# First weight sums of the down projections made in DRAM, and three more seven-product pairs

## The chip, the cores and the metric

The kernel runs on one core of one Trainium2 chip. The metric is the device time of one execution in microseconds (us); of several runs the median is given. A profile is one further execution, taken by the hardware profiler; its times are counted from the first instruction of the program. Engines: PE is TensorE (matmuls; PEld its weight loads), DVE is VectorE, ACT is ScalarE, POOL is GpSimd, SP is SyncE, which here only issues DMAs.

## The reference

A two-layer encoder trunk on 256 tokens of width 2048, in float32. Each layer has an attention sub-layer (token mixer and memory heads, one output projection) and an MLP:

```python
for i in range(DEPTH):                       # 2 layers
    h = rms_norm(x, norm_attn[i])
    ...                                      # input projection w_in_a or w_in_b, memory k/v, heads
    x = x + heads @ w_out[i]
    h = rms_norm(x, norm_mlp[i])
    x = x + jnp.square(jax.nn.relu(h @ w_up[i])) @ w_down[i]
```

`w_up` is 2048 x 8192 and `w_down` 8192 x 2048. The change concerns the product with `w_down`, and when its preparations are done.

## The kernel before, in words

**Products in three parts.** Every weight and every activation is split into a high part (a cast to float32r on ACT) and a low part (the difference, on DVE); a product is three matmuls: high x high, high x low, low x high. `split` (L411 to L413) is used for weights, activations and sums alike, so most of ACT's and DVE's work stands on L412 and L413.

**Pieces.** All weights come in pieces of 512 KB (128 partitions x 1024 floats) in the order of `plan`: layer by layer the input projection (`a` with 10 chunks of 8 pieces, `b` with 6), the memory projection (16 pieces), `out` (32), `up` (16 chunks of 8 pieces) and `down` (two halves of the output columns, each 32 pairs of 2 pieces). `piece` hands out the next piece and calls `fetch` so that two more are under way (AHEAD). `fetch` issues the load on SP (L389) into one of four raw buffers, and splits into one of four hi and four lo buffers. The framework's scheduler then puts each engine's instructions into an order at build time; at run time every engine works through its own in order, held up by semaphores.

**Pairs with seven products.** In `out` and `down` a pair of pieces is normally 8 groups of three matmuls (2 k-blocks x 2 token halves x 2 column chunks; `one_of_eight`). For the pairs listed in FAST (15 of 32), or LATE (13 of 32; layer 0, second half), `seven` does the same work in 7 groups, by Strassen's scheme. It needs sums of weight blocks: the first sum `a` (one block plus another broadcast over two, 128 x 1024) and two further halves `b` (L344, L345), which are then split like weights (`sum_pair`). It also needs differences of activations (`differences`, L515 to L518). These are made once for each hidden block j during `up`, saved to DRAM on GpSimd's queue by `keep` (tile `kept`), and loaded back on GpSimd's queue when pair j comes (L1038 in before).

**Where the first sums come from in before.** For 19 of the 58 fast pairs (MADE, MADE_LATE) `make_sum` makes the first sum ahead, during the first 13 chunks of `up`: three loads on SP (768 KB) into h2 and t2k tiles, the sum on DVE (L282, tile h), and a save of 512 KB in two parts on GpSimd's queue (L307, tile `madesum`). Such a pair later loads its sum (`big<-madesum`, L327) and only the half of the second piece that it still needs (`t2k<-in_w_down`). For the other 39 pairs `sum_pair` makes the sum on DVE (L282, big<-big) when the pair is fetched.

**Slots and the wait chains.** During `down`, raw pieces, first sums and second sums of the fast pairs live in six slots of one large tile (`big`). These are free once the hidden blocks of chunks 6 to 11 (AWAY) that were in them have been saved to DRAM on GpSimd's queue (tile `hid`, L987) and their differences taken. Loads into slots are issued on SP up to two pairs ahead (L324, L327, L333), in the same queue as all other weight loads. `bias_hot` (L796) gathers rows of a table on GpSimd's queue early in layer 0: eight groups of four DMAs, each read by DVE (L797) and then by matmuls (L806) that build the bias of the attention scores.

Of the kernel before, what the change touches and what calls it, by code (L numbers as in the profile page):

```python
# [22 lines left out]
P = 128  # L23
# [21 lines left out]
SINGLE = 4  # L45
AHEAD = 2
WARM = 10
FAST = (1, 3, 5, 7, 9, 11, 13, 15, 17, 19, 21, 23, 25, 27, 29)
LATE = (3, 5, 7, 9, 11, 13, 15, 17, 19, 21, 23, 25, 27)
AWAY = range(6, 12)  # L50
LATE_BLK = (9, 13, 17, 21, 25)
LOOK = 2
KEEP_AFTER = (2, 6)
MADE_GAP = 1
MADE = (3, 9, 15, 21, 27)
MADE_LATE = (7, 13, 19, 25)
LAM_INIT = 0.8 - 0.6 * math.exp(-0.3 * 0)

G_ATTN, G_MEM, G_MLP = 0, 2 * KT, 4 * KT
# [9 lines left out]
def trunk(ctx: ExitStack, tc: tile.TileContext, xin, xtok, memin, memtok, posrel, gcol, rows,  # L69
# [172 lines left out]
            return LATE if (name, h) == ("down0", 1) else FAST  # L242
        return ()

    def made_pairs(name, h):

        if name.startswith("down"):
            return MADE_LATE if (name, h) == ("down0", 1) else MADE
        return ()

    def plan_pairs(name, n):
        plan.extend((name, h, j) for h in range(2) for j in range(2 * n))

# [27 lines left out]
    def first_sum(a, first, upper):  # L281
        nc.vector.tensor_tensor(a, first.rearrange("p (a n) -> p a n", a=2), upper.unsqueeze(1).broadcast_to([P, 2, 512]), op=ALU.add)  # L282

    def make_sum(name, h, j):

        box = {}

        def load(i):
            if i == 0:
                box["raw"] = quad("h2", (P, 1024), F32), t2k([P, 512])  # L290
            first, upper = box["raw"]
            with tc.issue_after(behind[0].ins):
                if i < 2:
                    nc.sync.dma_start(first[:, i * 512:(i + 1) * 512], weights[name][h, 2 * j][:, i * 512:(i + 1) * 512])
                else:
                    nc.sync.dma_start(upper, weights[name][h, 2 * j + 1][:, 512:1024])

        def add():
            first, upper = box["raw"]
            box["a"] = quad("h2", (P, 2, 512), F32)  # L300
            box["kept"] = dp.tile([P, 2, 512], F32, name=nm("madesum"))
            first_sum(box["a"], first, upper)
            made_in[name, h, j] = box["kept"]
            save(0)

        def save(i):
            nc.gpsimd.dma_start(box["kept"][:, i, :], box["a"][:, i, :])  # L307

        return Task([lambda: load(0), lambda: load(1), lambda: load(2), add, lambda: save(1)], gap=MADE_GAP)

    made_in = {}
    hidden_in, hids = {}, {}
# [80 lines left out]
    def piece(name, c, j, lead=None):  # L393

        if lead is not None:
            fetch(2, lead)
            if j == 7:
                for _ in range(AHEAD):
                    fetch()
        else:  # L400
            while plan and len(ready) <= AHEAD:
                fetch()
        key, hi, lo = ready.popleft()
        assert key == (name, c, j), (key, name, c, j)
        return hi, lo

    def split_gain(hi, lo, src, g):
# [544 lines left out]
    def mlp(layer, X2, last):  # L952
# [13 lines left out]
            kept[j] = dp.tile([P, 2, 512], F32R, name=nm("kept"))  # L966
            nc.gpsimd.dma_start(kept[j], t2)

        to_make = [(f"down{layer}", h, j) for h in range(2) for j in made_pairs(f"down{layer}", h)]
        for c in range(16):  # L970
            for i in range(len(to_make) * c // 13, len(to_make) * (c + 1) // 13):
                if i < len(to_make):
                    make_sum(*to_make[i])
            ps = chunk_out(f"up{layer}", c, 8, lambda k: X2[k], "mm" if c % 2 == 0 else "aux", 2 if c == 0 else 1)
            if c == 0:
                mlp_stats()
            ht = wide[:, c - 6] if 6 <= c < 12 else blk([P, 4, S], F32)
            for o in range(4):
                t = t1k()
                nc.scalar.copy(t, ps[o][:, 256:512])  # L980
                nc.vector.tensor_tensor(t, ps[o][:, 0:256], t, op=ALU.add)
                nc.vector.scalar_tensor_tensor(ht[:, o, :], t, 0.0, t, op0=ALU.max, op1=ALU.mult)
            hT.append(ht)
            if c in AWAY:
                for i in range(2):
                    hidden_in[2 * c + i] = dp.tile([P, 512], F32, name=nm("hid"))
                    nc.gpsimd.dma_start(hidden_in[2 * c + i], hidden(2 * c + i))  # L987
            for j in (2 * c, 2 * c + 1):
                if any(j in fast_pairs(f"down{layer}", h) for h in range(2)):
                    Task([Light(lambda j=j: keep(j), 0)], wait=KEEP_AFTER[j % 2])  # L990
        N2 = Halves()

        def h2_of(j):
            t2 = quad("h2", (P, 2, 512))
# [5 lines left out]
        for half_ in range(2):  # L1000
            tag = "mm" if half_ == 0 else "aux"
            ps = [[bank(tag) for _ in range(2)] for _ in range(2)]
            chunks = (2 * half_, 2 * half_ + 1)
            fast = fast_pairs(f"down{layer}", half_)

            def add_to(n, t, src, i=0):
                at = chunks[n] * 512 + i
# [20 lines left out]
            for j in range(32):  # L1028
# [11 lines left out]
                else:  # L1040
                    for kk in range(2):
                        for t in range(2):
                            for n in range(2):
                                own_last = 2 * fast[-1] - 1 if last and half_ == 1 and n == t == 1 else 4 * KT - 1
                                one_of_eight(ps, n, t, 2 * j + kk, own_last, two, at)
                if j == fast[-1]:
                    shared(side, add_to)
# [45 lines left out]
    rows_done = [Task([lambda i=i: bias_hot(i), lambda i=i: bias_rows(i, bias)], [prep], wait=BW, gap=BGAP) for i in range(8)]  # L1093
    Task([lambda: bias_save(bias)], rows_done)
    H2 = Halves(lambda pair: "h2" if pair < 6 else "x2")
    loads = Task([lambda c=c: load_residual(c) for c in range(4)], wait=RES_AT, gap=RES_GAP, front=True)
    for g in range(3):
        if g == 2:
# [29 lines left out]
    st1 = cp.tile([P, 4], F32, name="st1")  # L1128
    H2 = Halves(lambda pair: "h2" if pair < 6 else "x2")
    bias = bias_load()  # L1130
    ps = chunk_tok("b", 3, X2, steps=2)
    row_stats(st1)
    kT, kd = norm_T(ps, st1, 4, gc[:, G_BK:G_BK + 1])
# [82 lines left out]
```

## Time and profile before

| what | value |
|---|---|
| median of 3 runs | 2094.53 us (2094.41 to 2095.34) |
| span of the profiled execution | 2092.7 us |
| median of the runs less that span | 1.8 us |
| granted TensorE clock, mean | 1.000 |
| matmul records, busy share of PE | 10920, 100% |
| busy share of DVE, ACT, POOL | 78%, 56%, 5% |
| DMA moved | 506.29 MB, mean 242 GB/s |

The groups of the page name line, engine, operation, written tile <- read tiles with shapes, count, busy time in us, mean ns of one, idle time before them and what ended it. The rows of the stages give for a stretch of the span the busy time of each engine, the granted clock, the mean busy share of the 16 DMA engines and the rate they moved. A wait row names who waited, for whom, the total in us, the number and the longest. Roughly: layer 0's input and memory projections with the heads run to about 320 us, then `out` to 414 us, `up` to 772 us, `down` to 1103 us; layer 1's to about 1308, 1403, 1761 and 2090 us.

### The profile page before, as it was taken

The numbers are of one execution on the slowest core, as the hardware profiler recorded it, in microseconds if no ns is written. First come the engines' busy times: TensorE is split into PE (matmuls) and PEld (weight loads), VectorE is DVE, ScalarE is ACT, GpSimd is POOL, SyncE is SP. The second block draws the span as 40 slices with busy tenths as digits, with TensorE's granted clock in tenths as the row PEclk, the third lists the DMA queues.
The fourth block names the chain that finished last, engine by engine and source line by source line (L and its number), as shares of the span: only waits on it lengthen the run. The fifth ranks groups of instructions, "written<-read, shape, count | busy, mean of one in ns | idle before, by whom it ended". The sixth has DMA issues, their size and how long they took to land.

```text
span 2092.7 us, 30004 instructions
## 1 busy us (share of the span) xinstructions
PE 2088.2 (100%) x10920; PEld 1773.8 (85%) x10920; DVE 1640.3 (78%) x2467; ACT 1173.6 (56%) x1776; POOL 103.0 (5%) x193
## 2 busy tenths in 40 slices
PE   9999999999999999999999999999999999999999
PEld 8888888888888888888888888888888888888887
DVE  7667778866666679999986677886676667999998
ACT  7467665544444456666655566564444445666664
POOL 1200000000011000000000000000010100000000
PEclk9999999999999999999999999999999999999999
DMA  9666654577789778878866555457788877888884
GB/s 320 241 204 200 194 161 161 186 241 251 251 298 310 238 264 274 293 246 268 303 243 197 178 171 178 149 194 250 252 272 299 307 231 277 273 288 289 284 294 145
DMA packets 150995, 506.29 MB, mean 242 GB/s; under 512 B 17856, under 2 KB 18880, under 8 KB 150592
## 3 DMA queue, kind: packets, MB, share of 16 engines
q1 hardware_dynamic: 131536, 437.78, 63.1%
q0 software_dynamic: 19168, 66.60, 9.5%
q8 instruction: 85, 1.39, 0.3%
q14 instruction: 62, 0.51, 0.1%
q10 hardware_dynamic: 144, 0.01, 0.0%
HBM read 466.96 MB, written 37.36 MB: 241 GB/s over the span
## 4 chain that ended last, share of the span: by engine, by line
PE 100%; DVE 0%; issue 0%
PE mm L478 11%; PE aux L478 11%; PE mm L465 7%; PE mm L466 7%; PE mm L467 7%; PE mm L505 7%; PE mm L506 7%; PE mm L504 7%; PE aux L506 7%; PE aux L505 7%; PE aux L504 7%; PE mm L482 6%; PE aux L482 6%; PE aux L600 1%; PE aux L577 1%; PE aux L619 1%
## 5 line engine op out<-in xcount | busy, mean ns | idle before, releaser
L413 DVE TENSOR_TENSOR lo<-raw,hi 128x1024 fp32r<-128x1024 f32 (+1 forms) x616 | 738.6, 1210 | 365.3 <-ACT hi L412 361.0
L412 ACT CAST hi<-raw 128x1024 fp32r<-128x1024 f32 (+1 forms) x616 | 632.0, 1040 | 592.4 <-PE mm L478 158.2
L465 PE MATMUL mm<-hi,x 128*128 128x512 f32 x640 | 256.5, 403 | 0.0
L466 PE MATMUL mm<-lo,x 128*128 128x512 f32 x640 | 251.3, 393 | 0.0
L467 PE MATMUL mm<-hi,x 128*128 128x512 f32 x640 | 250.4, 392 | 0.2 <-DVE x L409 0.2
L478 PE MATMUL mm<-x,hi 128*128 128x512 f32 x1024 | 246.9, 391 | 0.0
L478 PE MATMUL aux<-x,hi 128*128 128x512 f32 x1024 | 246.9, 391 | 0.0
L478 PEld LDWEIGHTS mm<-x,hi 128*128 128x128 f32 x1024 | 188.3, 188 | 36.3
L478 PEld LDWEIGHTS aux<-x,hi 128*128 128x128 f32 x1024 | 188.3, 188 | 36.3
L412 ACT CAST x<-big 128x1024 fp32r<-128x1024 f32 x106 | 110.6, 1053 | 141.6 <-DVE big L345 114.9
L504 PE MATMUL mm<-hi,h 128*128 128x512 f32 (+1 forms) x454 | 176.1, 388 | 0.0
L505 PE MATMUL mm<-lo,h 128*128 128x512 f32 (+1 forms) x454 | 176.0, 388 | 0.0
L506 PE MATMUL mm<-hi,h 128*128 128x512 f32 (+1 forms) x454 | 176.0, 388 | 0.0
L504 PE MATMUL aux<-hi,h 128*128 128x512 f32 x440 | 171.5, 390 | 0.0
L506 PE MATMUL aux<-hi,h 128*128 128x512 f32 x440 | 171.2, 390 | 0.0
L505 PE MATMUL aux<-lo,h 128*128 128x512 f32 x440 | 171.2, 389 | 0.0
L467 PEld LDWEIGHTS mm<-hi,x 128*128 128x128 f32 x640 | 120.3, 188 | 26.3 <-DVE x L409 0.5
L465 PEld LDWEIGHTS mm<-hi,x 128*128 128x128 f32 x640 | 120.6, 189 | 23.8
L466 PEld LDWEIGHTS mm<-lo,x 128*128 128x128 f32 x640 | 120.8, 189 | 23.0 <-DVE lo L413 1.0
L482 PEld LDWEIGHTS aux<-x,lo 128*128 128x128 f32 x1024 | 131.3, 191 | 5.0
L482 PEld LDWEIGHTS mm<-x,lo 128*128 128x128 f32 x1024 | 131.1, 191 | 4.8
L482 PE MATMUL mm<-x,lo 128*128 128x256 f32 x1024 | 133.0, 283 | 0.0
(270 smaller groups left out, 3101.8 us busy)
## 6 DMA issues: line engine op xcount, KB each, us to landing
raw<-in_w_up SPq DMA_DIRECT2D x256, 512.0 KB, 4.6
raw<-in_w_down SPq DMA_DIRECT2D x140, 512.0 KB, 4.7
big<-in_w_down SPq DMA_DIRECT2D x97, 512.0 KB, 5.0
raw<-in_w_a SPq DMA_DIRECT2D x72, 512.0 KB, 3.7
h<-kept POOLq DMA_DIRECT2D x58, 512.0 KB, 6.0
raw<-in_w_out SPq DMA_DIRECT2D x52, 512.0 KB, 4.0
raw<-in_w_b SPq DMA_DIRECT2D x48, 512.0 KB, 3.7
raw<-in_w_mem SPq DMA_DIRECT2D x32, 512.0 KB, 3.6
```

The source lines that it names most:

```text
L412: nc.scalar.copy(hi, src)
L413: return nc.vector.tensor_tensor(lo, src, as32(hi), op=ALU.subtract)
L465: nc.tensor.matmul(ps[t], lhsT=xh, rhs=hi[:, ws], start=(k == 0), stop=False)
L466: nc.tensor.matmul(ps[t], lhsT=xh, rhs=lo[:, ws], start=False, stop=False)
L467: nc.tensor.matmul(ps[t], lhsT=xl, rhs=hi[:, ws], start=False, stop=(k == KT - 1))
L478: nc.tensor.matmul(ps[o], lhsT=hi[:, cols(k % 2, o)], rhs=x2.rearrange("p a s -> p (a s)"), start=(k == 0), stop=(k == 2 * nj - 1))
L482: nc.tensor.matmul(ps[o][:, 256:512], lhsT=lo[:, cols(k % 2, o)], rhs=x2[:, 0, :], start=False, stop=False)
L504: nc.tensor.matmul(acc_, lhsT=x(0), rhs=w2[0][:, ws], start=first_, stop=False)
L505: nc.tensor.matmul(acc_, lhsT=x(0), rhs=w2[1][:, ws], start=False, stop=False)
L506: nc.tensor.matmul(acc_, lhsT=x(1), rhs=w2[0][:, ws], start=False, stop=last_)
L577: nc.tensor.transpose(out=pt[:, h * P:(h + 1) * P], in_=qn[t][:, h * P:(h + 1) * P], identity=ident)
L600: nc.tensor.transpose(out=pt[:, kt * S + qt * P:kt * S + (qt + 1) * P], in_=p_of(qt)[:, kt * P:(kt + 1) * P], identity=ident)
```

## The change

`make_sum`, its lists and its tasks go. `make_sums(layer)`, called at the start of each layer's input projection, lays down a list of steps, one every 5 consumed pieces before `up` and one every 10 in `up`, starting 26 pieces (layer 0) or 2 pieces (layer 1) after the call. A step issues two DMAs on GpSimd's queue: an add for the pair before, and a copy for the next pair. The copy goes from the weights in DRAM to a tile in DRAM (512 KB); the add reads half a piece twice (a broadcast, 512 KB in all) and adds it to the copy by the DMA's own accumulation. Each copy is given a dependency on the low-part split of the piece fetched last. All 61 fast pairs of the two down projections now find their first sum in DRAM; `sum_pair` makes one on DVE only for `out`. FAST gets 16 pairs in place of 15, with 9 and 10, and 18 and 19, next to each other; LATE stays. `own_last` is now worked out from the last pair that is not fast (28 in both kernels).

```diff
-FAST = (1, 3, 5, 7, 9, 11, 13, 15, 17, 19, 21, 23, 25, 27, 29)
+FAST = (1, 3, 5, 7, 9, 10, 12, 14, 16, 18, 19, 21, 23, 25, 27, 29)
 LATE = (3, 5, 7, 9, 11, 13, 15, 17, 19, 21, 23, 25, 27)
...
-MADE_GAP = 1
-MADE = (3, 9, 15, 21, 27)
-MADE_LATE = (7, 13, 19, 25)
+SUM_AT = {0: 26, 1: 2}
+SUM_GAP = 5
+SUM_GAP_UP = 10
...
+    def make_sums(layer):
+
+        name = f"down{layer}"
+
+        def copy(h, j):
+            made_in[name, h, j] = dp.tile([P, 2, 512], F32, name=nm("madesum"))
+            after_piece(nc.gpsimd.dma_start(made_in[name, h, j].rearrange("p a n -> p (a n)"), weights[name][h, 2 * j]))
+
+        def add(h, j):
+            upper = weights[name][h, 2 * j + 1][:, 512:1024]
+            nc.gpsimd.dma_start(made_in[name, h, j], upper.unsqueeze(1).broadcast_to([P, 2, 512]), accum_op=ALU.add)
+
+        def after_piece(ins):
+            tc.add_manual_dep(ins.ins, done[0].ins.name, mybir.DependencyInfo(mybir.DependencyClass.Sync, mybir.DependencyReason.DATA),
+                              reason="behind a piece")
+
+        def step(i):
+            if i:
+                add(*wanted[i - 1])
+            if i < len(wanted):
+                copy(*wanted[i])
+
+        wanted = [(h, j) for h in range(2) for j in fast_pairs(name, h)]
+        at = fetched[0] + SUM_AT[layer]
+        for i in range(len(wanted) + 1):
+            making.append((at, lambda i=i: step(i)))
+            at += SUM_GAP if at < before_up[layer] else SUM_GAP_UP
...
         key, hi, lo = ready.popleft()
         assert key == (name, c, j), (key, name, c, j)
+        fetched[0] += 1
+        while making and making[0][0] <= fetched[0]:
+            making.popleft()[1]()
         return hi, lo
...
-        to_make = [(f"down{layer}", h, j) for h in range(2) for j in made_pairs(f"down{layer}", h)]
         for c in range(16):
-            for i in range(len(to_make) * c // 13, len(to_make) * (c + 1) // 13):
-                if i < len(to_make):
-                    make_sum(*to_make[i])
...
         N2 = Halves()
+        while making:
+            making.popleft()[1]()
...
+            plain_last = max(j for j in range(fast[-1]) if j not in fast)
...
-                                own_last = 2 * fast[-1] - 1 if last and half_ == 1 and n == t == 1 else 4 * KT - 1
+                                own_last = 2 * plain_last + 1 if last and half_ == 1 and n == t == 1 else 4 * KT - 1
...
+    make_sums(0)
...
+    make_sums(1)
```

How the instructions move, first on GpSimd's queue in layer 0's attention, before. The rows name line, operation, written <- read tile and shape; blk<-bkt are the bias gathers:

```order
L796 DMA blk_1074<-bkt 32x2048 x4
L796 DMA blk_1098<-bkt 32x2048 x4
L796 DMA blk_1122<-bkt 32x2048 x4
L307 DMA madesum_4961<-h_4960 128x512 x2
L967 DMA kept_5016<-h_5009 128x1024
```

The same place in the changed kernel (L284 the copy, L288 the add, L798 the gathers):

```order
L798 DMA blk_1074<-bkt 32x2048 x4
L284 DMA madesum_1086<-in_w_down 16x8192
L798 DMA blk_1100<-bkt 32x2048 x4
L798 DMA blk_1124<-bkt 32x2048 x4
L288 DMA madesum_1086<-in_w_down 256x1x512
L284 DMA madesum_1309<-in_w_down 16x8192
L288 DMA madesum_1309<-in_w_down 256x1x512
```

The first copy stands ahead of the last two groups of gathers, and from the second sum on each add stands right behind its own copy.

GpSimd's queue in layer 0's `up`, chunks 6 and 7, before (hid<-big is the save of a hidden block that frees a slot):

```order
L987 DMA hid_6138<-big_4621 128x512
L987 DMA hid_6140<-big_4621 128x512
L307 DMA madesum_6240<-h_6239 128x512 x2
L967 DMA kept_6295<-h_6288 128x1024
L987 DMA hid_6357<-big_4621 128x512
L987 DMA hid_6359<-big_4621 128x512
```

And in the changed kernel:

```order
L284 DMA madesum_6078<-in_w_down 16x8192
L288 DMA madesum_6078<-in_w_down 256x1x512
L985 DMA hid_6187<-big_4683 128x512
L985 DMA hid_6189<-big_4683 128x512
L969 DMA kept_6246<-h_6239 128x1024
L969 DMA kept_6343<-h_6336 128x1024
L284 DMA madesum_6352<-in_w_down 16x8192
L288 DMA madesum_6352<-in_w_down 256x1x512
L985 DMA hid_6408<-big_4683 128x512
L985 DMA hid_6410<-big_4683 128x512
```

The saves of both chunks now stand behind a copy and its add, where before a save of a made sum stood between them.

More of the change, by code (lines that the diff above doesn't have):

```diff
@@ L243, in fast_pairs @@
         return ()
[L245 to L249, printed above, removed]
     def plan_pairs(name, n):
@@ L282, in first_sum @@
         nc.vector.tensor_tensor(a, first.rearrange("p (a n) -> p a n", a=2), upper.unsqueeze(1).broadcast_to([P, 2, 512]), op=ALU.add)
[L284 to L309, printed above, removed]
+    def make_sums(layer):
[19 more added lines that the diff above has]
+            at += SUM_GAP if at < before_up[layer] else SUM_GAP_UP
@@ L311, in trunk @@
+    making = deque()
+    fetched = [0]
+    before_up = [i for i, (name, c, j) in enumerate(plan) if name.startswith("up") and (c, j) == (0, 0)]
     made_in = {}
```

## The prediction

> **What bounds the kernel now.** I read the page's busy times first, then the chain of waits, then the timeline of TensorE, then the stages, then who waits for whom.
>
> ```profile
> span 2092.7 us, 30004 instructions
> PE 2088.2 (100%) x10920; PEld 1773.8 (85%) x10920; DVE 1640.3 (78%) x2467; ACT 1173.6 (56%) x1776; POOL 103.0 (5%) x193
> PE 100%; DVE 0%; issue 0%
> ```
>
> TensorE is busy for the whole span and the chain that ended last is TensorE alone. A busy TensorE may still be a slow one, so I looked at the pace. The timeline of TensorE inside the first down projection has these two rows as first and last of 55 consecutive matmuls:
>
> ```profile
> 899.69 0.39 PE L504 MATMUL mm<-hi,h 128*128 128x512 f32 x1
> ...
> 911.93 0.39 PE L504 MATMUL mm<-hi,h 128*128 128x512 f32 x1
> ```
>
> 54 steps in 12.24 us are 0.2267 us for a matmul of 512 columns, and in those rows no matmul starts late. The stages (a piece of the load-heavy start, layer 0's attention, layer 0's down projection, layer 1's up projection) say the same: PE's busy time equals the stretch in each, while the DMA share differs widely. Columns: stretch, length, then PE, PEld, DVE, ACT, POOL busy with counts, clock, DMA share, GB/s.
>
> ```profile
> 20.00:30.00 10.00, 10.00 (x46) 8.29 (x45) 9.19 (x21) 6.16 (x12) 0.09 (x1) 1.00 1.04 398
> 100.00:370.00 270.00, 270.00 (x1455) 222.84 (x1454) 205.19 (x498) 169.37 (x374) 0.00 (x0) 1.00 0.56 184
> 780.00:920.00 140.00, 140.00 (x619) 115.95 (x618) 130.72 (x148) 90.19 (x111) 6.86 (x13) 1.00 0.84 279
> 1560.00:1680.00 120.00, 120.00 (x695) 106.25 (x694) 82.10 (x117) 54.93 (x73) 14.52 (x27) 1.00 0.88 301
> ```
>
> DVE in the down projection is at 130.7 of 140 us, close to becoming the bound, but it isn't: TensorE's work has no hole there. So the kernel is a queue of matmuls; time goes down only by removing matmuls, and goes up if anything starves TensorE.
>
> How much starving it stands is told by the waits (engine, line, releaser: total us, times, longest):
>
> ```profile
> SPq L389 <- DVE lo L413: 1042.2, 458, 12.2
> ACT hi L412 <- PE mm L478: 158.2, 90, 2.7
> ACT hi L412 <- DMA raw<-in_w_down: 8.2, 2, 8.0
> ```
>
> The weight loads on SP wait for a raw buffer to be split, and the split waits for TensorE to free a hi buffer. Both rings are full; hardly anything waits for a landing. From the loads of w_a, and from the up projection's chain, the period of a piece:
>
> ```profile
> L389 SPq DMA_DIRECT2D raw<-in_w_a x43: 327/328/328, 100.0 to 243.4; - x43
> DMA to landing us min/median/max: 3.2/3.6/10.4
> 423.91 3.65 PE mm L478 x16
> 427.56 1.91 PE mm L482 x16
> 429.48 3.65 PE mm L478 x16
> raw<-in_w_up SPq DMA_DIRECT2D x256, 512.0 KB, 4.6
> ```
>
> A piece takes (243.4 - 100.0)/42 = 3.41 us in attention and (429.48 - 423.91)/2 = 2.78 us in up. With four raw buffers a load has four periods from issue to the end of its split.
>
> **The change part by part.**
>
> *Matmuls.* A plain pair is 8 groups of 3 matmuls, a seven-product pair 7 groups. Three more fast pairs (one in layer 0, two in layer 1) are 3 x 3 = 9 matmuls less. 9 x 0.2267 = 2.04 us, all on the path. This is the only term on the path that I can name.
>
> *Vector and scalar work.* The groups by line, with their shapes:
>
> ```profile
> L282 DVE TENSOR_TENSOR big<-big 128x1024 f32<-128x1024 f32 x39 | 47.5, 1219 | 0.0
> L282 DVE TENSOR_TENSOR h<-h,t2k 128x1024 f32<-128x1024 f32 x19 | 23.2, 1219 | 0.0
> L344 DVE TENSOR_TENSOR big<-big 128x512 f32<-128x512 f32 x58 | 39.8, 686 | 0.1
> L413 DVE TENSOR_TENSOR x<-big,x 128x1024 fp32r<-128x1024 f32 x106 | 129.4, 1221 | 0.5 <-ACT x L412 0.5
> L413 DVE TENSOR_TENSOR h<-t2k,h 128x512 fp32r<-128x512 f32 x78 | 51.7, 687 | 13.1 <-ACT h L412 13.1
> ```
>
> All 58 first sums leave DVE: 47.5 + 23.2 = 70.7 us. Three pairs come: 3 x (2 x 0.69 + 2 x 1.22) = 11.4 us. Six more hidden blocks get their differences (five in layer 0, whose two halves now use different blocks, and one in layer 1): four instructions of at most 0.69 us, 6 x 2.8 = 17 us at most, in up. Net about -42 us of DVE, worth 0, since TensorE doesn't wait for DVE. It matters as cover: two neighbouring fast pairs (9 and 10, 18 and 19) ask of DVE 2 x (1.22 + 0.69 + 2 x 0.69 + 2 x 1.22 + 0.69) = 12.8 us, while TensorE needs 2 x 21 x 0.2267 = 9.5 us: a deficit of 3.3 us. The old unmade pair alone had 7.6 against 4.8 us, a deficit of 2.8 us, and was covered, so I put 0 here too; if that cover fell short, it would be by about 0.5 us at each of six places.
>
> *DMA.* This is the term that can hurt. The queues, and GpSimd's nearest 512 KB transfer:
>
> ```profile
> q1 hardware_dynamic: 131536, 437.78, 63.1%
> q0 software_dynamic: 19168, 66.60, 9.5%
> h<-kept POOLq DMA_DIRECT2D x58, 512.0 KB, 6.0
> ```
>
> q0: 0.095 x 2092.7 = 199 us of all 16 engines for 66.6 MB, so 1.57 us for 512 KB (q1 gives 1.58). No row shows a copy from DRAM to DRAM or an adding DMA. Lower end: each counts as one pass, 2 x 1.57 = 3.1 us for a sum. Upper end: the transfers hold the engines for their whole 6.0 us to landing, once for the copy and twice for the add (it reads 512 KB of weights and 512 KB of the copy), 18 us. I take one pass and two passes at q0's rate, 4.7 us, since q0 is the same queue and the same engines.
>
> The old sums cost 768 KB of loads and 512 KB of saves, 3.9 us each. In attention a sum comes every five pieces, 17.1 us: share 0.56 + 4.7/17.1 = 0.83. In up, ten pieces, 27.8 us: an old sum came about every 30 us, so 0.88 - 3.9/30 + 4.7/27.8 = 0.92. In down, 42 more pairs load a sum of 512 KB in place of half a piece, 0.8 us each, and three more load kept differences: 42 x 0.8 + 3 x 1.6 = 38 us over 128 pairs of some 5.1 us, which takes 0.84 to 0.90. Every stage stays below 1, so I put 0; the reserve for bursts is 4 x 3.41 - 3.6 - 2.3 = 7.7 us in attention and 4 x 2.78 - 4.6 - 2.3 = 4.2 us in up (2.3 us: cast and split), plus the lead of the splits.
>
> The Trainium skill, "DMA: Bandwidth & Descriptors", section "Issuing engines are not separate DMA queues", speaks against the change: a DMA issued from GpSimd runs on the same 16 engines as SP's. The trace agrees: both queues are given as shares of the same engines. Had GpSimd's queue engines of its own, the shares of 0.83 and 0.92 would be the old 0.56 and 0.75.
>
> *Waits added on GpSimd.* A copy waits for a split, and the order shows that the add stands right behind its copy, so it waits for the copy's landing and not five pieces. Behind them are the bias gathers (once), and in up the saves of kept and hid. Nobody on the path waits for these unless they come some us late: rivals B and C.
>
> Sum: -2.04 us. Profiled span 2092.7 - 2.04 = 2090.7 us; the median of the runs stands 1.8 us above the span, so **2092.5 us**.
>
> **Rivals.**
>
> *A, slower: the DMA engines fill up.* It decides where a sum costs over (1 - 0.56) x 17.1 = 7.5 us in attention, or (1 - 0.75) x 27.8 = 7.0 us in up. Priced with five passes, each crossing of DRAM one (copy two, add three), 7.9 us: over by 0.4 x 40 sums in attention and 0.9 x 21 in up, 35 us, less a reserve of about 8 us in each layer, +19 us. 2094.5 - 2.0 + 19 = 2111.5 us. At the far end of 18 us it would be hundreds. Against it: q0's rate, and the row at 20 us, where 398 GB/s were moved. For it: no row shows an add. By bytes, up would move 301 - 1.31 MB/30 us + 2.62 MB/27.8 us = 351 GB/s, below those 398.
>
> The Trainium skill, "HBM Reference", section "Specifications (TRN2)", gives about 358 GB/s as a core's share; by it up would be 98% full and A's chance nearer 0.2. The row of 398 GB/s exceeds that share, so the measurement decides and I keep 0.10.
>
> *B: a wait chain through GpSimd in up.* The save of a hidden block (hid) stands behind copy and add; it frees the slot that SP's next prefetch for down waits for, and up's weight loads stand behind that prefetch. Before, in layer 0:
>
> ```profile
> 598.05 0.54 POOL L987 DMA_DIRECT2D hid<-big  x1 [0.79 <-DVE big L982]
> ...
> 603.49 0.33 SPq L333 DMA_DIRECT2D big<-in_w_down  x1
> ```
>
> The copy ahead of it waits for the split of the next chunk's first piece, which ends before that chunk starts; I take 590 us, an estimate from the save's own time. Landing after 6.0 us, the add goes at 596 us and the save is on time. If copies take 12 us, the save is 4 to 6 us late, and up's reserve of 4.2 us is just used up. Some 2 us at two slots in each layer: 2.0 less gained, +4 to +8, about 2098 us.
>
> *C: the bias gathers.* The first copy stands ahead of the last eight gathers and waits for a split. Rows of DVE in order of time, and the gathers' own:
>
> ```profile
> 79.92 1.22 DVE L413 TENSOR_TENSOR lo<-raw,hi 128x1024 fp32r<-128x1024 f32 x1
> ...
> 92.21 0.75 DVE L797 TENSOR_SCALAR blk<-blk,itf 128x2048 bf16<-128x2048 bf16 x1
> ...
> 95.82 0.74 DVE L797 TENSOR_SCALAR blk<-blk,itf 128x2048 bf16<-128x2048 bf16 x1
> L796 POOL DMA_DIRECT2D blk<-bkt x32 | 17.5, 549 | 30.9 <-DMA bkt<-t1k 24.7 <-DMA blk<-bkt 5.3 <-issue 0.4
> blk<-bkt POOLq DMA_DIRECT2D x32, 128.0 KB, 5.6
> ```
>
> From 81.1 us: nine issues of 0.55 us and 5.6 us to land end at 91.7 us, the first four gathers at 89.5 us. Their readers started at 95.8 and 92.2 us: 2.7 us in hand. A late landing by 5 us would cost some 2 us of TensorE: 2094.5 us.
>
> **How the numbers follow.** Forecast 0.71, A 0.10, B 0.11, C 0.05; 0.03 for a gain beyond the nine matmuls, which no row supports. 0.2% of 2094.5 us, about what a measurement of this kernel can tell from no change, is 4.2 us: the forecast's 2.0 us lie within. Slower by more than that: A, half of B and a fifth of C, 0.16. Faster: 0.03. Same: 0.81. The range goes from 2091.4 us (the forecast less 1.1 us, the spread of the three runs and a little) to 2099 us, which takes in C, the larger part of B and the 3 us of the neighbouring pairs, and leaves out A.
>
> **What would show it right or wrong.** Right: PE still 100% of the chain, span near 2090.7 us, no rows of L282 on DVE but those of the output projection, DVE in down below 130 of 140 us, DMA share near 0.83 in layer 0's attention and near 0.92 in layer 1's up. A shows as casts (ACT hi) that wait for DMA raw in attention or up, and PE short of the stretch there; B as long waits of SP at the prefetch lines in up with GpSimd's hid saves late; C as a hole of TensorE near 95 to 103 us. The forecast is wrong if TensorE has holes of over 6 us in sum, or if its pace of 0.2267 us changes.

## The result, and the profile after

| | before | after |
|---|---|---|
| median of 5 runs each, us | 2094.71 (2094.41 to 2095.34) | 2104.17 (2102.36 to 2107.12) |
| ratio, 95% interval | 1 | 1.0048 (1.0036 to 1.0061) |
| span of the profiled execution, us | 2092.7 | 2102.4 |

The change makes the kernel slower, by 9.5 us from median to median and by 0.48% by the ratio of the runs; the prediction was 2092.5 us, at most 2099. Nine matmuls fewer should have given 2.0 us, so 11.7 us were lost in the profiled execution. The page of the changed kernel:

```profile
span 2102.4 us, 30141 instructions
...
PE 2091.8 (99%) x10911; PEld 1770.9 (84%) x10911; DVE 1588.5 (76%) x2445; ACT 1183.2 (56%) x1788; POOL 185.7 (9%) x286
...
PE 96%; DMA 1%; DVE 1%; issue 1%; ACT 0%; SPq 0%; DVEq 0%; ACTq 0%
...
q1 hardware_dynamic: 129376, 433.85, 60.7%
q0 software_dynamic: 35968, 125.32, 22.1%
...
madesum<-in_w_down POOLq DMA_DIRECT2D x122, 512.0 KB, 6.4
raw<-in_w_a SPq DMA_DIRECT2D x72, 512.0 KB, 5.2
```

The chain is no longer TensorE alone: DMA, DVE and issue hold some 3% of it. GpSimd's queue went from 9.5% to 22.1% of all 16 DMA engines, and the pieces of w_a land after 5.2 us instead of 3.7. The chain holds four transfers, all of them loads issued on SP (start, length):

```profile
4.50 6.50 DMA xs<-in_xin
...
390.84 6.79 DMA blk<-in_w_out
...
1045.22 7.30 DMA big<-madesum
...
1267.89 6.86 DMA h<-in_memin
```

Four places, then: the very start (before the first copy), the seven-product pairs of layer 0's `out`, layer 0's `down`, and the memory's features in layer 1's memory projection. The stages around them follow, and those the prediction spoke of (100 to 370, 780 to 920 and 1560 to 1680 us stand beside the rows quoted there):

```profile
95.00:103.00 8.00, 8.00 (x123) 6.64 (x119) 4.07 (x6) 2.93 (x5) 1.46 (x2) 1.00 0.77 254
100.00:370.00 270.00, 270.00 (x1454) 222.50 (x1453) 205.58 (x497) 168.39 (x372) 24.73 (x32) 1.00 0.81 243
780.00:920.00 140.00, 139.94 (x616) 115.25 (x615) 123.23 (x143) 92.96 (x114) 7.41 (x14) 1.00 0.87 298
1560.00:1680.00 120.00, 120.00 (x692) 106.08 (x691) 73.80 (x107) 53.62 (x69) 16.33 (x25) 1.00 0.93 298
...
320.00:414.00 94.00, 92.58 (x445) 76.95 (x445) 76.64 (x111) 51.88 (x84) 9.27 (x12) 1.00 0.78 229
937.00:1103.00 166.00, 165.07 (x733) 135.74 (x733) 140.82 (x165) 102.57 (x134) 11.31 (x14) 1.00 0.81 281
1248.00:1290.00 42.00, 39.22 (x196) 33.04 (x195) 33.49 (x81) 27.12 (x59) 3.62 (x5) 0.96 0.76 229
```

The last three in the kernel before:

```profile
320.00:414.00 94.00, 94.00 (x456) 79.22 (x455) 79.70 (x114) 51.40 (x84) 0.00 (x0) 1.00 0.52 170
937.00:1103.00 166.00, 166.00 (x743) 137.65 (x741) 151.06 (x174) 103.91 (x135) 9.38 (x14) 1.00 0.80 273
1248.00:1290.00 42.00, 41.84 (x218) 35.26 (x217) 35.95 (x88) 27.69 (x60) 0.00 (x0) 1.00 0.55 177
```

On average no stage has its DMA engines full, and the fullest, up at 0.93, leaves TensorE without a gap. TensorE starves where the mean share is only 0.76 to 0.81, and where before it was busy for 94.00 of 94, 166.00 of 166 and 41.84 of 42 us. But the mean of a stage hides what one load meets. Over the 6.79 us in which the chain's load of `out` was under way (from 390.84 us) the share was 1.00; over the same load before (5.00 us from 389.99 us) it was 0.66. For the memory's features (6.86 us from 1267.89 us) it was 0.93, before (4.84 us from 1261.53 us) 0.77. What was late in each stage is told by who waited for landings, most of all in these rows:

```profile
ACT blk L414 <- DMA big<-madesum: 16.7, 5, 5.1
...
ACT hi L414 <- DMA blk<-in_w_out: 10.2, 4, 6.0
...
ACT x L410 <- DMA h<-in_memin: 5.1, 2, 3.2
```

and by the timeline at the longest hole, where ACT makes x from the memory's features:

```profile
1274.78 0.91 ACT L410 ACTIVATE x<-h,gc 128x256 fp32r<-128x256 f32 x2 [3.16 <-DMA h<-in_memin]
...
1275.34 0.58 PE L467 MATMUL mm<-hi,x 128*128 128x512 f32 x1 [2.78 <-ACT x L410]
...
1275.72 0.63 PE L468 MATMUL mm<-lo,x 128*128 128x512 f32 x1
...
1276.14 0.63 PE L467 MATMUL mm<-hi,x 128*128 128x512 f32 x1
```

The load was issued at 1267.89 us, 0.12 us after a copy on GpSimd's queue (at 1267.77 us), took 6.86 us, and TensorE stood idle for 2.78 us.

To compare runs I added up, for each stage of a profiled execution, by how much the starts of neighbouring matmuls lie more than 0.227 us apart (only where they are more than 0.3 us apart, so that matmuls at a slower pace count too), less the same of the kernel before. For the changed kernel: `out` of layer 0 2.2 us, layer 1's attention and memory 3.9, `down` 2.5 and 1.2, layer 1's `out` 0.2, `up` none: 10.0 us. The start lost about another 0.9 us; no run ties that to the change, since it varies from -0.3 us (e7) to 1.1 us (e2) and is 0.6 us in e1 without any copies. The remaining 0.8 us lie in no step that counts. The table below has these "holes" beside the medians; they are those of one execution, whose time can lie off the median (e1's took 2098.06 us). One of the eleven executions of e15 took 7455 us, and without it its median is 2097.35 us.

### The profile page after: what moved, and what is told of

The parts are those of the page before. It is cut to its first block, busy times and chain, and to the rows that moved or that the text cites. A ratio compares the mean times of both kernels' runs of the same rounds, so it can differ in the third digit from the quotient of the medians.

```text
span 2102.4 us, 30141 instructions
## 1 busy us (share of the span) xinstructions
PE 2091.8 (99%) x10911; PEld 1770.9 (84%) x10911; DVE 1588.5 (76%) x2445; ACT 1183.2 (56%) x1788; POOL 185.7 (9%) x286
## 3 DMA queue, kind: packets, MB, share of 16 engines
q0 software_dynamic: 35968, 125.32, 22.1%
## 4 chain that ended last, share of the span: by engine, by line
PE 96%; DMA 1%; DVE 1%; issue 1%; ACT 0%; SPq 0%; DVEq 0%; ACTq 0%
PE mm L480 11%; PE aux L480 11%; PE mm L467 7%; PE mm L468 7%; PE mm L469 7%; PE mm L508 6%; PE mm L507 6%; PE mm L506 6%; PE aux L508 6%; PE aux L507 6%; PE aux L506 6%; PE mm L484 6%; PE aux L484 6%; PE aux L602 1%; PE aux L579 1%
## 5 line engine op out<-in xcount | busy, mean ns | idle before, releaser
L414 ACT CAST hi<-raw 128x1024 fp32r<-128x1024 f32 (+1 forms) x610 | 625.5, 1040 | 652.1 <-PE aux L480 166.1
L507 PE MATMUL mm<-lo,h 128*128 128x512 f32 (+1 forms) x443 | 171.7, 388 | 0.0
L506 PE MATMUL mm<-hi,h 128*128 128x512 f32 (+1 forms) x443 | 171.7, 388 | 0.0
L508 PE MATMUL mm<-hi,h 128*128 128x512 f32 (+1 forms) x443 | 171.4, 388 | 0.1
L415 DVE TENSOR_TENSOR x<-big,x 128x1024 fp32r<-128x1024 f32 x112 | 136.3, 1218 | 0.0
```

The source lines that it names most:

```text
L414: nc.scalar.copy(hi, src)
L415: return nc.vector.tensor_tensor(lo, src, as32(hi), op=ALU.subtract)
L506: nc.tensor.matmul(acc_, lhsT=x(0), rhs=w2[0][:, ws], start=first_, stop=False)
L507: nc.tensor.matmul(acc_, lhsT=x(0), rhs=w2[1][:, ws], start=False, stop=False)
L508: nc.tensor.matmul(acc_, lhsT=x(1), rhs=w2[0][:, ws], start=False, stop=last_)
```

## Experiments

Theory **T1**: the copies and additions lengthen all other loads by 1 to 2 us; weight pieces have a reserve for that, but some loads are issued just in time and pass it on to TensorE. Rivals: **T2**, the new pairs and the loads of their sums in `down` cost nearly all; **T3**, GpSimd's waits and order; **T4**, the copy's long packets (32 KB; 16 of them for 512 KB) block the others.

| kernel | median, us | to before (95%) | holes: out 0 | attention and memory 1 | down 0 | down 1 |
|---|---|---|---|---|---|---|
| changed | 2104.17 | 1.0048 (1.0036 to 1.0061) | 2.2 | 3.9 | 2.5 | 1.2 |
| e1 no sums made | 2096.25 | 1.0009 (1.0000 to 1.0018) | 0.0 | -0.1 | 4.2 | 1.2 |
| e4 copies only | 2098.81 | 1.0018 (1.0009 to 1.0027) | 0.6 | 0.8 | 2.6 | 1.2 |
| e3 4 KB rows | 2105.53 | 1.0051 (1.0038 to 1.0063) | 2.6 | 2.1 | 2.3 | 1.2 |
| e2 old pairs | 2104.81 | 1.0050 (1.0036 to 1.0063) | 2.8 | 4.4 | 2.1 | 0.0 |
| e7 pairs alone | 2094.51 | 0.9998 (0.9989 to 1.0007) | 0.0 | 0.2 | 0.6 | 0.9 |
| e8 traffic alone | 2103.09 | 1.0040 (1.0028 to 1.0052) | 3.0 | 4.2 | 0.0 | 0.0 |
| e15 the same, none in mem, out | 2097.68 | 1.0013 (1.0004 to 1.0022) | 0.0 | 1.4 | 0.0 | 0.0 |
| e5 none in mem, out | 2100.09 | 1.0027 (1.0017 to 1.0037) | 0.0 | 1.3 | 5.7 | 1.2 |
| e6 memory early | 2101.45 | 1.0042 (1.0030 to 1.0054) | 2.8 | 0.2 | 3.4 | 1.2 |
| e9 late half by DVE | 2104.09 | 1.0045 (1.0032 to 1.0058) | 2.0 | 6.5 | 1.1 | 1.2 |
| e13 e9 and e6 | 2100.69 | 1.0026 (1.0015 to 1.0037) | 2.0 | 2.0 | 1.6 | 1.2 |
| e14 e1, late half by DVE | 2095.34 | 1.0003 (0.9993 to 1.0012) | 0.0 | 0.0 | 0.8 | 1.2 |
| e12 seven 2 KB buffers | 2105.74 | 1.0049 (1.0036 to 1.0063) | 3.8 | 5.6 | 4.1 | 1.2 |
| e10 mended, 52 sums | 2098.47 | 1.0015 (1.0006 to 1.0024) | 0.0 | 3.0 | 0.6 | 1.2 |
| e11 mended, 19 sums | 2094.05 | 0.9997 (0.9988 to 1.0006) | 0.0 | -0.2 | 0.7 | 0.8 |

**Is it the traffic, and what of it?** e1 leaves the copies and additions out, with the same loads in `down`:

```diff
-            made_in[name, h, j] = dp.tile([P, 2, 512], F32, name=nm("madesum"))
-            after_piece(nc.gpsimd.dma_start(made_in[name, h, j].rearrange("p a n -> p (a n)"), weights[name][h, 2 * j]))
+            made_in[name, h, j] = weights[name][h, 2 * j].rearrange("p (a n) -> p a n", a=2)
...
-            nc.gpsimd.dma_start(made_in[name, h, j], upper.unsqueeze(1).broadcast_to([P, 2, 512]), accum_op=ALU.add)
+            pass
```

> The changed kernel without the 61 copies and 61 additions from DRAM to DRAM; the down projection loads the first half's weight piece where it would have loaded the sum, so its loads and matmuls are the same in number and size and the sums that they use are the wrong numbers. Theory T1 (the copies and additions lengthen every load by 1 to 2 us, and the loads that are issued with no reserve pass that on to TensorE): the holes of the attention and out stages go (about 2.3 us in the first out stage, 4.0 in the second attention), those at the down stages' fast pairs (2.6 and 1.2 us, where no copy runs) stay: 2096 to 2098 us. Rival T2 (the down stages alone, by their three more and neighbouring pairs and the just-in-time loads of the sums, cost nearly all): 2102 to 2104 us. Rival T3 (GpSimd's waits and the order of its queue delay the saves and bias steps): like T1 here, but then the landings of the weight pieces needn't fall back to 3.7 to 4.6 us.

2096.25 us: 7.9 of the 9.5 us are the traffic's. The loads land as before again; the rows of the pieces of w_a and of the memory's features in e1:

```profile
raw<-in_w_a SPq DMA_DIRECT2D x72, 512.0 KB, 3.9
...
h<-in_memin SPq DMA_DIRECT2D x8, 512.0 KB, 4.9
```

Before it was 3.7 and 4.9 us, in the changed kernel 5.2 and 6.1 (the pieces of w_up rose from 4.6 to 4.8 only, so "all other loads by 1 to 2 us" says too much). That speaks for T1 and against T3, by which these needn't fall, and which doesn't fit a chain whose transfers are all SP's; T2 isn't the bulk, but `down` keeps its holes. e4 keeps the copies and drops the additions:

```diff
-            nc.gpsimd.dma_start(made_in[name, h, j], upper.unsqueeze(1).broadcast_to([P, 2, 512]), accum_op=ALU.add)
+            pass
```

> The changed kernel with the 61 copies but without the 61 additions: the first weight piece stands where the sum would. T1 by bytes and packet time (the packets of a copy take 1.29 us of each DMA engine, those of an addition 16 x 0.21 = 3.4 us): the loads are lengthened by about a third of what they were, 2097 to 2100 us. T4 (the copy's long descriptors block the rest): the whole loss of the stages before down stays, 2101 to 2104 us.

2098.81 us: the additions cost 5.4 us, the copies 2.6. The share of GpSimd's queue in e1 and in e4,

```profile
q0 software_dynamic: 17424, 61.35, 8.4%
```

```profile
q0 software_dynamic: 19376, 93.34, 12.2%
```

gives the price of each (their spans are 2096.3 and 2096.6 us): (0.122 x 2096.6 - 0.084 x 2096.3)/61 = 1.3 us of all engines for a copy, (0.221 x 2102.4 - 0.122 x 2096.6)/61 = 3.4 us for an addition. The loss of time (2.6 and 5.4 us, 1 to 2.1) roughly follows these prices (1 to 2.6). e3 cuts a copy into 4 KB packets:

```diff
-            made_in[name, h, j] = dp.tile([P, 2, 512], F32, name=nm("madesum"))
-            after_piece(nc.gpsimd.dma_start(made_in[name, h, j].rearrange("p a n -> p (a n)"), weights[name][h, 2 * j]))
+            rows = dp.tile([P, 1040], F32, name=nm("madesum"))
+            made_in[name, h, j] = rows[:, 0:1024].rearrange("p (a n) -> p a n", a=2)
+            after_piece(nc.gpsimd.dma_start(rows[:, 0:1024], weights[name][h, 2 * j]))
```

> The changed kernel with the sums kept in DRAM in rows of 1040 numbers, of which 1024 are used, so that a copy is no longer one run of 512 KB and its descriptors are 4 KB (128 rows) instead of 32 KB (16). T4 (a 32 KB descriptor holds an engine for 1.29 us in one piece, and the loads queue behind it): the loads land 1 us sooner and most of the holes of attention and out go: 2096 to 2099 us. T1 (what counts is the bytes and the time of all packets, most of it the additions' 2 KB ones): 2102 to 2106 us.

GpSimd's packets rose from 35968 to 42800 (61 x 112 more), the time not at all down: 2105.53 us. T4 is out. Whether the other loads wait for the DMA engines themselves or for the DRAM behind them, no run separates.

**The pairs and the traffic apart.** e2 puts the old FAST into the changed kernel, e7 the new FAST into the kernel before (e7's edit):

```diff
-FAST = (1, 3, 5, 7, 9, 11, 13, 15, 17, 19, 21, 23, 25, 27, 29)
+FAST = (1, 3, 5, 7, 9, 10, 12, 14, 16, 18, 19, 21, 23, 25, 27, 29)
...
-MADE = (3, 9, 15, 21, 27)
+MADE = (3, 10, 14, 19, 25)
...
```

> The changed kernel with the fifteen odd pairs of before in the down projections (58 seven-product pairs, none beside each other); all 58 sums are still made from DRAM to DRAM on GpSimd's queue. T1: the stages ahead of down keep their holes; the matmuls come back (+2.04 us) and the small holes at neighbouring pairs (about 0.5 us at six places by the trace) go: 2102 to 2106 us, that is no change worth naming against the changed kernel. T2: the down stages lose their holes: 2095 to 2097 us.

> The kernel before with the changed kernel's seven-product pairs alone (61 instead of 58, two neighbouring pairs in three of the four halves); the first sums are made as before, by VectorE, five of them per half ahead of time (now those of pairs 3, 10, 14, 19 and 25). By the change's own account: 9 matmuls fewer (-2.04 us) and about 0.3 us lost at each of six neighbouring places (+1.8 us): 2094 to 2095.5 us. Rival T2 (the neighbouring pairs are what the down stages can't bear): 2097 us and more.

Both within what T1 said. The pairs alone are worth -0.3 us, not -2.0: at each of the six neighbouring places TensorE waits about 0.2 to 0.3 us, 0.6 + 0.9 us in sum. e8 is the reverse, the kernel before with 58 idle copies and additions beside it (`make_sums` as in the change, its tiles never read):

> The kernel before, whose down projections stay as they were (58 pairs, sums by VectorE), with the changed kernel's copies and additions from DRAM to DRAM on GpSimd's queue beside it (58 of each, at the same weight pieces), whose results nothing reads. T1: the loss of the stages ahead of down alone, 2.3 + 4.0 + 0.2 us and up to 0.9 us at the start: 2100 to 2102.5 us. If the traffic hurts only through the down stages' loads of the sums: 2095 to 2096 us.

2103.09 us, 0.6 above what T1 gave: 8.3 us from traffic that nobody uses, and none in `down`, where none of it runs. Its holes, with 1.1 us in layer 1's `out`, add up to the same 8.3 us. Its up projection, where TensorE has no hole at a DMA share of 0.98, beside its out projection:

```profile
320.00:414.00 94.00, 91.85 (x442) 76.43 (x441) 75.93 (x109) 51.13 (x83) 9.28 (x12) 1.00 0.78 231
...
1560.00:1680.00 120.00, 120.00 (x689) 105.99 (x689) 77.20 (x107) 52.86 (x68) 20.14 (x32) 1.00 0.98 337
```

So neither the mean share of a stage nor the total decides, but which loads stand in the stage. e15 leaves the 19 of 58 sums out that fall due in the memory and output projections; e5 does the same to the changed kernel (there `down` loads the weight piece instead, so those sums are wrong):

```diff
         def copy(h, j):
+            if now[0].startswith(("mem", "out")):
+                left_out.append((h, j))
+                return
...
```

> The kernel before with the copies and additions beside it whose results nothing reads (2103.09 us with all 58), without those that fall due in the memory and output projections. T1: only those two stages lack reserve: 2095 to 2097 us. If the cost goes by the total of the traffic: two thirds of 8.3 us remain, about 2100 us.

> The changed kernel, but the 19 of its 61 sums that fall due in the memory and output projections of the two layers are left out (no copy, no addition; the down projection loads the first half's weight piece in their place, so those sums are the wrong numbers); the other 42 are made where they were. T1 (only loads without reserve pass a longer landing on, and these are the features of the memory in the memory projection and the seven-product pairs' loads in the output projection): the holes there go (2.3 us in the first output projection, 2.8 us at the memory features of the second layer, 0.2 us in the second output projection), what the down stages lose stays: 2098 to 2100.5 us. If instead the traffic costs by its total, wherever it lies: a third of the 8 us that it was measured to cost (2104.2 less 2096.25), 2101 to 2102 us.

A third of the traffic carried 5.4 of 8.3 us (e15: 2097.68 us; 0.7 above T1's range, 2.3 below the rival's) and 4.1 us in the changed kernel (e5: 2100.09 us). `out` lost nothing any more. 1.3 to 1.4 us stayed at the memory's features; no copy or addition was under way at that hole, but the last sums that fell due before the memory projection had run on into it.

**The memory's features.** e6 loads them two pieces earlier:

```diff
...
+            if j == 0:
+                load(0)
             if j % 2 == 0:
-                raw = quad("h2", (P, 4, S), F32)
-                nc.sync.dma_start(raw, memin[:, 512 * j:512 * j + 1024].rearrange("p (k s) -> p k s", s=S))
+                load(j + 2)
...
```

> The changed kernel with all its sums, but the memory's features are loaded two weight pieces earlier in the memory projections (about 5.4 us of reserve more for three of four loads). T1: the hole of 2.8 us at the fifth piece of the second layer's memory projection goes, everything else stays: 2100 to 2102.5 us. If the DMA engines as such were the bound there, the next weight piece would be late instead: 2103.5 to 2105 us.

2101.45 us: by the medians 2.7 us come back, and in the profile the stage's holes shrink from 3.9 to 0.2 us, with no cast waiting for a weight piece behind them. But two of e6's five executions took 2106 and 2108 us, so that the time saved isn't clear of the scatter.

The reserve is also eaten from the other side: the load stands in SP's queue behind weight pieces, which wait for VectorE's splits. In the kernel before it was issued at 1261.53 us and TensorE came up short at 1268.2, 6.7 us later (by 0.2 us); in the changed kernel 1267.89 and 1272.3, 4.4 us, and in e5 1268.33 and 1272.7, 4.4 us too. A later issue as well as a longer landing, then, and the rows divide them. From the issue of the memory projection's first weight piece to that of this load it is 29.2 us in the kernel before and in e1, 30.5 in the changed kernel, 30.9 in e5 and 31.0 in e15. The load lands after 4.8 us before, 6.9 in the changed kernel, 5.5 in e5 and 5.4 in e15. So it comes 1.2 + 2.0 = 3.2 us later than before in the changed kernel, and 1.7 + 0.6 = 2.3 us later in e5 and e15; ScalarE waited 3.2 and 2.2 us for it. The later issue too goes with the traffic: in e5 and e15 the last addition was issued at 1255.42 and 1251.44 us, inside the memory projection, the two feature loads ahead of this one landed after 6.6 to 7.3 us instead of 5.2 and 5.3, and ScalarE waited 2.4 us for the first of them instead of 0.5. That this wait is what puts off the pieces and the load behind them is read from the rows; no run took it away alone.

**The first `down`.** From 950 us on its chain of waits goes, in e1, round by round from VectorE's split to the next load and back:

```profile
980.91 5.11 DMA t2k<-hid
986.02 1.04 ACT hi L412
...
988.23 1.22 DVE lo L413
...
989.96 1.23 DVE lo L413
991.21 5.68 DMA big<-in_w_down
997.08 1.22 DVE lo L413
```

A load waits for the buffer that VectorE's split frees, and that split waits for the load before. In e9 nine of the thirteen pairs of that half (LATE) get their sum from VectorE again; e13 adds the early features, e14 is the same edit without any traffic:

```diff
-        wanted = [(h, j) for h in range(2) for j in fast_pairs(name, h)]
+        wanted = [(h, j) for h in range(2) for j in fast_pairs(name, h) if (layer, h) == (1, 1) or h == 0 or j in MADE_LATE]
```

> The changed kernel, but in the second half of the first layer's down projection (pairs 3 to 27) only four of the thirteen sums are made from DRAM to DRAM and loaded, as in the kernel before; the other nine are made by VectorE at their pair again, from the whole second piece. T1 with the closed loop that the chains of the runs show there (a pair's load waits until VectorE's split has freed its buffer, lands 5 to 7 us later, and ScalarE's split and VectorE's work on it stand ahead of the next load): the holes of that half go (1.4 us and more in the profiles), the rest stays: 2101 to 2103 us, with under 1 us of holes in the first down projection. If the three more pairs were the cause: nothing changes there, 2103.5 to 2105 us.

> The changed kernel with both edits: nine of thirteen sums of the first down projection's second half made by VectorE at their pair again, and the memory's features loaded two pieces earlier. If the two losses are separate and the earlier run's unchanged median came from a longer hole at the memory's features: 2098.5 to 2101 us, less than the 2101.45 us of the earlier loads alone. If the sum loads of that half cost nothing in most executions: 2101 to 2102.5 us.

> The kernel without copies and additions (2096.25 us, sums replaced by weight pieces, so that the output is made of wrong sums), and in the first down projection's second half nine of the thirteen pairs without the load of a sum: VectorE makes them. If the loop of loads in that half is what keeps that kernel above the 2094.5 us of the pairs alone: 2093.5 to 2095 us, with under 1 us of holes in the first down projection. If not: 2095.5 to 2097 us.

e9 missed, and came out in the range of its rival (2104.09 us): the half's holes shrank (2.5 to 1.1 us), but the time stayed, with a longer stop at the memory's features (6.5 us). With those loads earlier too (e13: 2100.69 us, though its profile has a stop of 2.4 us in that stage again, behind VectorE) the edit gives 0.8 us beyond e6, and without traffic (e14: 2095.34 us, between the two ranges) 0.9 us beyond e1. By the medians, then, the sum loads of that half cost just under 1 us, which the scatter of e1 and e6 doesn't separate from nothing. The profiles show holes of 2.1 to 5.7 us in that stage where the sums are loaded. These are single executions, and the loop doesn't cost the same in each: e1's eleven spread over 7.6 us, e14's over 1.0. e12 asked which buffers close the loop:

```diff
-        return tp.tile(shape, dt, tag="t2k", name=nm("t2k"), bufs=6)
+        return tp.tile(shape, dt, tag="t2k", name=nm("t2k"), bufs=7)
...
-        return tp.tile([P, 256], F32, tag="t1k", name=nm("t1k"), bufs=4)
+        return tp.tile([P, 256], F32, tag="t1k", name=nm("t1k"), bufs=3)
```

> The changed kernel with seven instead of six of the 2 KB buffers that hold the second piece's half and the hidden features on their way back (and three instead of four of the 1 KB ones, to make room). If these small buffers close the loop of the first down projection's second half: its holes go, 2101.5 to 2103 us. If the 4 KB slots of the pieces and sums do (SP's waits at the load of the sum, 16.7 us against 7.6 at the two small loads): no change, 2103 to 2105.5 us.

2105.74 us and holes of 4.1 us: one more 2 KB buffer doesn't help, though the 1 KB buffer given up for it may have cost something; more room for the 4 KB slots wasn't tried.

**Mending it.** e10 is e13 with 52 sums and none begun in the memory and output projections; e11 makes only 19, all in `up`:

```diff
...
+            if at < before_up[layer] and names[at].startswith(("mem", "out")):
+                at = before_up[layer] + 2
...
```

> The last kernel with 52 sums from DRAM to DRAM, the memory's features two weight pieces earlier, and no sum begun in the memory and output projections (the ones that fell there are spread over attention and up: every 4th piece in the second attention, every 6th in the second up projection). T1: all the holes named so far go except the six small ones at neighbouring pairs; 2094.8 - 2.0 + 1.8 and up to 1.5 us at the start and in rest: 2095 to 2097.5 us, unless the second up projection's reserve doesn't bear a sum every 6 pieces (a sum takes 4.7 us of 14.5 us there, where the engines are already 0.79 to 0.94 busy): then 2100 us and more, with holes in that stage. If the traffic cost by its total: 2102 us.

> 61 pairs as in the changed kernel, but only 19 sums from DRAM to DRAM (five of each half, four of the late one), all of them made during the up projections, one per 11 weight pieces, the others by VectorE at their pair; the memory's features are loaded two pieces earlier. T1: the up projections' weight pieces have the reserve for it, no stage without reserve is touched: 2093.5 to 2095.5 us, the same as the kernel before. If a sum costs wherever it lies (8 us for 61 copies and additions): 2096.5 to 2097.5 us.

e11 comes out at 2094.05 us, the same as before (ratio 0.9997): nineteen sums beside `up` are free within the interval, with 0.4 us of holes in its first `up`. e10 misses its range by 1.0 us. Its memory projection has a hole of 1.8 us again, but now behind VectorE (why VectorE is late there stays open), and its second `up`, with a sum every 6 pieces and the DMA engines 0.99 busy, the chain of rival B:

```profile
1636.67 10.01 DMA hid<-big
...
1647.18 7.62 DMA raw<-in_w_up
```

The save of a hidden block takes 10.0 us to land, SP's prefetch waits for it, a weight load behind it comes late, and TensorE loses 0.9 us. No version was faster than the kernel before.

## Why the prediction was wrong, point by point

- **The step that failed** is the one on the DMA engines: "Every stage stays below 1, so I put 0; the reserve for bursts is 4 x 3.41 - 3.6 - 2.3 = 7.7 us in attention and 4.2 us in up". Its parts were right: 4.7 us of all engines for a sum (measured 1.3 + 3.4), shares of 0.83 and 0.92 (0.81 and 0.93; `down` 0.87 against 0.90), and weight pieces that bear it. But the reserve was worked out for the weight pieces with their four buffers alone, and a stage's mean share was taken for what each load meets. The memory's features and the seven-product pairs of `out` have no such ring; their loads are issued just in time, landed after 4.9 and 5.0 us (medians) and now land after 6.1 and 6.7. The term put at 0 measured 7.9 us (changed less e1) and 8.3 us (e8); e15 and e5 show that most of it hangs on the memory and output projections. That the ring is what protects the weight pieces is argued from `up`; no run took buffers away. The trace before already had the warning: the prediction read only waits for weight pieces (`raw`), and the same list has these, each a load that came no earlier than it was needed:

```profile
ACT blk L412 <- DMA big<-madesum: 3.2, 2, 1.6
...
ACT hi L412 <- DMA blk<-in_w_out: 1.4, 2, 0.9
...
ACT x L408 <- DMA h<-in_memin: 0.5, 1, 0.5
```

- **The matmuls**: the pairs alone gave -0.3 us, not -2.04 (e7). The cover at neighbouring pairs, put at 0, fell short by about 1.5 us of holes: the text had it as up to 0.5 us at six places; it is 0.2 to 0.3.
- **`down`**: the loads of the sums were counted as 0.8 us of engine time each. What they cost by the medians is 1.7 us in all (e1 less e7): just under 1 us by a wait in a closed loop in the late half (e14, within the scatter), and 0.8 us by which e14 still stands above e7, unexplained.
- The sum as it should have been, from the runs: pairs -0.3 (e7), sum loads +1.7 (e1 less e7), traffic +7.9 (changed less e1), 9.3 us of the 9.5 measured. These are steps from one run to the next and so must add up; the check is e8, which has the traffic at 8.3 us by itself.
- **Rival A** did not happen as it was priced: on average no stage is full, and `up` stood 0.98 in e8. Its sign did show, casts that waited for weight pieces in `up` (12 times, 25.4 us in all), but TensorE had no hole there. **B** happened only when sums came every 6 pieces instead of every 10 (e10). **C** did not: TensorE is busy from 95 to 103 us. No rival named loads without a ring. The sign of failure that was given, holes of over 6 us in sum, is what came.
- VectorE's relief of 52 us, from 1640.3 to 1588.5, bought nothing that a run shows, as said.

## What to carry to other kernels

Transfers added "in the background" are to be priced by what they do to the landing of every other load in their stage: list for each stage the loads that aren't in a deep ring, with issue, landing and first use, before putting a DMA term at 0. The mean share of busy engines doesn't tell it: 0.98 was free in a stage of ringed weight pieces (e8), 0.78 cost 2 to 3 us in one with loads just in time. If such transfers are wanted, they go where only ringed loads run (e11), and not too densely (e10).

## What the runs showed of the hardware that was not expected

**A long stop costs more than itself.** After the 2.78 us at 1272 us the next matmuls of 512 columns came 0.43 us apart (1275.72, 1276.14 in the rows above) instead of 0.227, with the granted clock at 0.58 over the four microseconds from 1275 us:

```profile
1275.00:1279.00 4.00, 3.66 (x10) 2.92 (x11) 2.82 (x9) 3.72 (x12) 0.00 (x0) 0.58 1.00 295
1279.00:1290.00 11.00, 11.00 (x55) 9.24 (x54) 8.06 (x21) 6.55 (x12) 0.51 (x1) 1.00 0.53 131
```

Taken over 1275.61 to 1279.02 us alone, 3.41 us, the granted clock is 0.50. From 1275.34 to 1279.20 us nine matmuls of 512 columns and one of 256 took 3.86 us; at 0.227 us each they would have taken 2.16, so about 1.7 us come on top of 2.8. The same followed stops of 2.9 us (e2), 3.0 us (e8) and 1.8 us (e10), but not those of 2.5 us in e3 and in e13, nor those of 1.5 us and less that stood alone. It also followed stops of at most 0.8 us that came close together, as in e5's first `down`:

```profile
1034.60:1038.00 3.40, 3.22 (x9) 2.39 (x8) 3.40 (x6) 1.49 (x4) 0.00 (x0) 0.55 0.92 313
```

The Trainium skill, "TensorE: Matmul & The Clock Gate", section "Part 1: The HAM clock gate", has the array at half rate after at least one idle window of about 3.4 us, with matmuls of 512 columns 426.7 ns apart, and gives as a rule no idle gaps over about 3.4 us. The pace and the length agree, but 1.8 to 3.0 us of idleness did it in four runs here, so that the rule is too generous for this kernel. What decides between the stops that did it and those that didn't stays open.

**An addition in DRAM costs 2.6 times a copy**, 3.4 against 1.3 us of all engines for 512 KB, and the size of a copy's packets (32 or 4 KB) made no difference to the time that the runs can tell. Both sit in the same engines as every load: the landings of w_a rose from 3.7 to 5.2 us with engines 0.81 busy. The Trainium skill, "DMA: Bandwidth & Descriptors", section "SWDGE vs HWDGE vs iDMA", says that an engine alternates between the two kinds of queue. The longer landings agree with that, though no run separates it from a wait in the DRAM.
